# Attention rows measured over all but the last two steps of the current heads, and their transposition made a step of its own

## The chip, the cores and the metric

The kernel runs on one core of a Trainium2 chip. The metric is the device time of one execution in microseconds (us). Of an execution that was profiled, the span from the first to the last instruction of the program is known as well.

## What is computed

The reference is one layer of a hybrid decoder trunk over 1024 prompt tokens and 8 x 8 sample tokens: a norm, one input projection, sparse attention beside a gated recurrence, an output projection and a squared-ReLU MLP. The change concerns two of the three attention branches of the prompt, which the kernel runs as plain causal softmax attention (the selected blocks are all blocks here) and as a window of 512 keys, each with a linear distance bias:

```python
s = jnp.einsum('bnqgrd,bnkgd->bngrqk', qg, kb) * SCALE - slopes * dist
s = jnp.where(ok, s, NEG)
p = jax.nn.softmax(s, axis=-1)
o = jnp.einsum('bngrqk,bnkgd->bnqgrd', p, vb)
...
o_a = gates[..., 0:1] * o_cmp + gates[..., 1:2] * o_sel + gates[..., 2:3] * o_win
```

## The kernel before

The engines are named as the profile names them: PE (matrix products; PEld its weight loads), DVE (vector), ACT (activations), POOL (GpSimd) and SP (which issues DMAs). A large product is written as three products of rounded halves, hi x hi, lo x hi and hi x lo, at L136, L137 and L138.

**Groups.** A group (i, g) is one block of 128 queries (i from 0 to 7) and four of the eight heads (g is 0 or 1). There are 16, in this order: (0,0), (1,0), (2,0), (0,1), (1,1), (2,1), then (7,0), (7,1), (6,0), (6,1), (5,0), (5,1), (4,0), (4,1), (3,0), (3,1).

**Measuring.** `measure` finds, for each query row of a group, the maximum and the logarithm of the sum of its exponentials, for two branches. A step of it makes a tile of scores (PE, L841 to L846), takes its maximum (DVE, L847, tile `mxs`) and sums its exponentials (ACT, L849, tile `sms`). Its last step joins the parts (DVE L856 to L860 and ACT L858 for i of 4 and more), takes the logarithm (ACT L861), subtracts it and the gate's logarithm (DVE L862, L863), splits the result into a rounded half and the rest (DVE L866, L867, tile `rr`), transposes that (PE L869, tile `tr`) and writes it into the tile `A2` (DVE L870; the page writes it `A`). With these rows in `A2`, the products that follow give exponents that need no further normalising.

**Values.** `values` then goes over the keys of the group. Its first step transposes the small compressed probabilities (PE L907). Each further step makes scores with the keys on the partitions (PE L915, L916, at a mask L918; L916 reads `A2`), takes the exponential (ACT L920), splits it in two (L922 on ACT and DVE in turn, L923 two times in three on POOL and else on DVE), and multiplies both halves with the values into the tile `O` (PE L896, L897). These two products stand four steps back, in a queue `pend`.

**Weaving.** `attend` walks over the groups. While the value steps of a group run, the measuring steps of the next one are dealt out among them. `n0` is the number of value steps (3 for i = 0, 14 for i = 7), `n1` that of the measuring steps (3 for i = 0, 17 for i of 4 and more). After each value step and each measuring step `fill` pulls products of work that does not depend on the attention (the recurrence's output projection, then the output projection and MLP of the first 384 tokens) as PE's filling. Queries of the group after the next one are prepared at the loop's start (DVE L957 to L959) and their compressed probabilities too (PE L803, DVE L807 to L815).

**Order.** The code's order is a priority, not the order on the engines: a scheduler places each instruction by priority as soon as by its own cost model it is ready, and `fill` raises the priority of the filling. Each engine then goes through its queue strictly in the order that results. Score tiles have three PSUM banks (`SC`), `tr` has two, `O` one. After the loop, `flush` ends the queue, and the samples and the MLP follow.

Of the kernel before, what the change touches and what calls it, by code (L numbers as in the profile page):

```python
# [39 lines left out]
FEATS = ((0,), (1,), (2,), (3, 4, 5), (6, 7))  # L40
SC, TRB, MMB = 3, 2, 2
LEAD = 44
LOOK = 4
FILL0 = (2600, 0)
FILL1 = (900, 1500, 20000)
# [5 lines left out]
def trunk(ctx: ExitStack, tc: tile.TileContext, I, O):  # L51
# [12 lines left out]
    def tl(p, shape, dt=F32, tag="t", bufs=None):  # L64
        return p.tile(shape, dt, tag=tag, name=nm(tag), bufs=bufs)
# [756 lines left out]
    def measure(i, g, A1, A2):  # L822
# [30 lines left out]
        else:  # L853
# [11 lines left out]
        hi, lo = (rr[:, :, :, j].rearrange("p h b -> p b h") for j in range(2))  # L865
        V.tensor_copy(hi, nmx)  # L866
        V.tensor_tensor(lo, nmx, hi.bitcast(F32), op=ALU.subtract)  # L867
        pt = tl(ps, [128, 128], tag="tr", bufs=TRB)
        PE.transpose(pt[:16], rr.rearrange("p h b j -> p (h b j)").bitcast(F32), ident)  # L869
        V.tensor_tensor(A2[96:], pt[:16, None, :].to_broadcast([16, 4, 128]), hsel[:, :, None].to_broadcast([16, 4, 128]),  # L870
                        op=ALU.mult)
        yield

    pend = deque()

# [13 lines left out]
    def values(po, i, g, A1, A2, pcm, fill, then):  # L889
# [11 lines left out]
        for si, st in enumerate(steps):  # L901
# [22 lines left out]
            fill(0)  # L924
            later(partial(weigh, si, m, vst, ph, pl), LOOK)
            yield
# [37 lines left out]
    def attend(groups, fills, out, ready):  # L964
# [29 lines left out]
        for x, (i, g) in enumerate(groups):  # L994
            nxt = iter(())
            fill = fills[i >= NQ0]
            if x + 1 < len(groups):
                after = ready.pop(0)
                nxt = measure(*groups[x + 1], *after[:2])
                n1 = steps_of(groups[x + 1][0])  # L1000
                if x + 2 < len(groups):
                    ready.append(soon(*queries(*groups[x + 2])))
            else:
                n1 = 0
            po = lazily(lambda: tl(ps, [128, 4, 128], tag="O"))
            og = lazily(partial(place, i, g))
            work = values(po, i, g, *cur, fill, partial(finish, po, og, i, g))
            n0 = 2 * i + 3 - span(i, 1)
            done = 0
            for k in range(n0):  # L1010
                next(work, None)
                while done < n1 and (done + 1) * n0 <= (k + 1) * n1:
                    next(nxt, None)
                    fill(1)
                    done += 1
            for _ in work:
                pass
            for _ in nxt:
                fill(1)
            if x + 1 < len(groups):  # L1020
                cur = after
# [224 lines left out]
    for x, _ in enumerate(cg):  # L1246
        if x >= LEAD and x % 4 == 0:
            next(lead, None)
# [19 lines left out]
    n0, n1 = NQ0 * 128, T - NQ0 * 128  # L1268
# [218 lines left out]
```

## Time and profile before

| what | us |
|---|---|
| median of 3 timed runs | 1673.99 |
| lowest and highest of them | 1669.6, 1679.21 |
| the profiled execution | 1668.53 |
| its span, first to last instruction | 1666.9 |
| PE busy in the span | 1602.3 |
| DVE, ACT, POOL busy | 958.6, 731.0, 365.4 |

A busy PE is a PE with a product in flight; a product's own duration overlaps the next one's. The stretch of the groups lies between 455 and 935 us after the span's start. A row of the timeline gives start, duration, engine, line, operation, tiles written and read, shapes and count; the bracket at its end is the engine's idle time before it and what ended that.

### The profile page before, as it was taken

To read this page: it belongs to the slowest core of one execution; us is meant where nothing else is said; L and a number is where in the kernel's file an instruction comes from. 1 tells how busy PE (TensorE), PEld (TensorE's weight loads), DVE (VectorE), ACT (ScalarE), POOL (GpSimd) and SP (SyncE) were. 2 spreads that over 40 slices of the span, in tenths; PEclk is the share of its full clock that TensorE was granted. 3 is DMA by queue.
4 is the path that set the end of the run, shared out by engine and by line. 5 is a ranking of instruction groups with operands and counts; after the bars stand their busy time and mean duration, and the time that the engine had idled before them with its cause. 6 is when DMAs were issued, how large, how long until landed. Compare 5 with 4: busy or idle time off the path is not lost.

```text
span 1666.9 us, 26555 instructions
## 1 busy us (share of the span) xinstructions
PE 1602.3 (96%) x10009; PEld 1462.6 (88%) x10009; DVE 958.6 (58%) x1785; ACT 731.0 (44%) x1546; POOL 365.4 (22%) x322
## 2 busy tenths in 40 slices
PE   8999999998799999999999999999999999999999
PEld 6798989998677787878877778999999999999998
DVE  6245656655477888887787555565543443443442
ACT  5334544444356778666677433334321221211211
POOL 0011303304124455332233201012220120110110
PEclk9999999999799999999999999999999999999999
DMA  5332232227745332221211475445222222122222
GB/s 198 120 73 78 72 97 94 60 73 211 215 134 154 121 116 76 70 76 62 67 55 39 146 223 170 140 145 178 73 68 69 71 64 76 64 64 76 76 81 77
DMA packets 131856, 171.79 MB, mean 103 GB/s; under 512 B 33642, under 2 KB 76714, under 8 KB 131722
## 3 DMA queue, kind: packets, MB, share of 16 engines
q1 hardware_dynamic: 128810, 160.71, 31.4%
q0 software_dynamic: 2912, 9.32, 1.8%
q8 instruction: 81, 1.33, 0.3%
q14 instruction: 53, 0.43, 0.1%
HBM read 141.62 MB, written 28.84 MB: 102 GB/s over the span
## 4 chain that ended last, share of the span: by engine, by line
PE 58%; DVE 9%; issue 3%; DMA 3%; ACT 2%; SPq 2%; POOL 0%; DVEq 0%; ACTq 0%; POOLq 0%
PE mm L136 14%; PE mm L137 14%; PE mm L138 14%; DVE wl L109 2%; PE tr L915 2%; PE tr L916 1%; PE sc L286 1%; PE sc L841 1%; DVE mxs L847 1%; PE O L896 1%; PE sc L842 1%; PE O L897 1%; DMA cm<-cache_c 1%; ACT sc L849 1%; PE sc L1084 1%
## 5 line engine op out<-in xcount | busy, mean ns | idle before, releaser
L108 ACT CAST wh<-ws 128x512 fp32r<-128x512 f32 x294 | 170.1, 618 | 385.1 <-PE mm L137 271.8
L136 PE MATMUL mm<-ah,wh 128*128 128x352 f32 (+1 forms) x744 | 249.7, 336 | 0.0
L109 DVE TENSOR_TENSOR wl<-ws,wh 128x512 fp32r<-128x512 f32 x268 | 218.7, 853 | 52.4 <-ACT wh L108 51.5
L137 PE MATMUL mm<-al,wh 128*128 128x352 f32 (+1 forms) x744 | 243.5, 327 | 0.0
L138 PE MATMUL mm<-ah,wl 128*128 128x352 f32 (+1 forms) x744 | 243.2, 327 | 0.0
L136 PE MATMUL mm<-uh,wh 128*128 128x352 f32 (+1 forms) x720 | 238.6, 331 | 0.0
L138 PE MATMUL mm<-uh,wl 128*128 128x352 f32 (+1 forms) x720 | 235.2, 327 | 0.0
L137 PE MATMUL mm<-ul,wh 128*128 128x352 f32 (+1 forms) x720 | 234.8, 326 | 0.0
L1227 POOL TENSOR_TENSOR sq<-r 128x352 f32<-128x352 f32 (+1 forms) x96 | 98.8, 1029 | 561.8 <-DVE r L1225 556.4
L923 POOL TENSOR_TENSOR pl<-e,ph 128x512 fp32r<-128x512 f32 x88 | 117.1, 1336 | 210.5 <-ACT ph L922 109.0
L136 PE MATMUL mm<-X,wh 128*128 128x364 f32 (+1 forms) x480 | 162.5, 339 | 0.0
L138 PE MATMUL mm<-X,wl 128*128 128x364 f32 (+1 forms) x480 | 158.5, 330 | 3.9 <-PEq L740 3.9
L137 PE MATMUL mm<-X,wh 128*128 128x364 f32 (+1 forms) x480 | 158.5, 330 | 0.0
L137 PEld LDWEIGHTS mm<-al,wh 128*128 128x128 f32 x744 | 140.2, 188 | 4.8 <-issue 3.2
L136 PEld LDWEIGHTS mm<-ah,wh 128*128 128x128 f32 x744 | 140.8, 189 | 1.5
L138 PEld LDWEIGHTS mm<-ah,wl 128*128 128x128 f32 x744 | 139.8, 188 | 1.9 <-issue 1.6
L137 PEld LDWEIGHTS mm<-ul,wh 128*128 128x128 f32 x720 | 135.6, 188 | 2.4 <-issue 1.6
L136 PEld LDWEIGHTS mm<-uh,wh 128*128 128x128 f32 x720 | 135.9, 189 | 1.8 <-issue 0.8
L138 PEld LDWEIGHTS mm<-uh,wl 128*128 128x128 f32 x720 | 135.3, 188 | 1.6 <-issue 1.2
L1239 DVE TENSOR_TENSOR H<-H,mm 128x352 f32<-128x352 f32 (+1 forms) x90 | 47.7, 530 | 154.1 <-PE mm L138 152.4
L849 ACT ACTIVATE sc<-sc,mxs 128x320 f32<-128x320 f32 (+5 forms) x192 | 100.8, 525 | 63.0 <-DVE mxs L847 60.1
L1225 DVE SCALAR_TENSOR_TENSOR r<-mm,rs 128x352 f32<-128x352 f32 (+1 forms) x93 | 49.7, 534 | 118.2 <-PE mm L138 117.6
(408 smaller groups left out, 3309.1 us busy)
## 6 DMA issues: line engine op xcount, KB each, us to landing
ws<-w_up SPq DMA_DIRECT2D x128, 256.0 KB, 2.8
ws<-w_down SPq DMA_DIRECT2D x128, 256.0 KB, 2.9
w<-w_feat SPq DMA_DIRECT2D x40, 256.0 KB, 2.9
ws<-w_or SPq DMA_DIRECT2D x22, 256.0 KB, 3.3
w<-cmp_w SPq DMA_DIRECT2D x8, 512.0 KB, 7.0
ws<-w_oa SPq DMA_DIRECT2D x16, 256.0 KB, 3.2
pgs<-cache_s SPq DMA_DIRECT2D x32, 128.0 KB, 3.3
cw<-cwin SPq DMA_DIRECT2D x8, 512.0 KB
```

The costliest lines, as they stand in the source:

```text
L108: A.copy(wh, w)
L109: (eng or V).tensor_tensor(wl, w, wh.bitcast(F32), op=ALU.subtract)
L136: PE.matmul(p, wh, zh, start=i == 0, stop=False)
L137: PE.matmul(p, wh, zl, start=False, stop=False)
L138: PE.matmul(p, wl, zh, start=False, stop=i == n - 1)
L286: PE.matmul(ph2[:, :161], w1[w][s // 8][:, s % 8], cm[:, w, :, s], start=s == 0, stop=s == 31)
L849: A.activation(sc[:, x], sc[:, x], AF.Exp, bias=mxs[:, br, h, c:c + 1], accum_out=sms[:, br, h, c:c + 1])
L915: PE.matmul(pt, B1[:, br, g, ks], A1, start=True, stop=False)
L923: (G if turn_[0] % 3 < 2 else V).tensor_tensor(pl, e, ph.bitcast(F32), op=ALU.subtract)
L1225: V.scalar_tensor_tensor(r[:, :n], p[:, :n], 0.0, rs2[:, sl], op0=ALU.max, op1=ALU.mult)
L1227: G.tensor_tensor(sq[:, :n], r[:, :n], r[:, :n], op=ALU.mult)
L1239: V.tensor_tensor(H[:, m, sl], H[:, m, sl], p[:, :n], op=ALU.add)
```

## The change

In `measure`, the `yield` that ended the last step now stands before the transposition. So the statistics end a step, and the transposition with the write of `A2` is one more step. In `attend`, the measuring steps are dealt out over `n0 - AHEAD` value steps, with `AHEAD = 2`; `n1` still counts one step beside the score tiles, so the loop runs all up to the statistics, and the transposition is run by the `for _ in nxt` loop behind the last value step. That generator ends there without a further `yield`, so no `fill` belongs to it.

```diff
 LEAD = 44
+AHEAD = 2
 LOOK = 4
...
         V.tensor_copy(hi, nmx)
         V.tensor_tensor(lo, nmx, hi.bitcast(F32), op=ALU.subtract)
+        yield
         pt = tl(ps, [128, 128], tag="tr", bufs=TRB)
         PE.transpose(pt[:16], rr.rearrange("p h b j -> p (h b j)").bitcast(F32), ident)
         V.tensor_tensor(A2[96:], pt[:16, None, :].to_broadcast([16, 4, 128]), hsel[:, :, None].to_broadcast([16, 4, 128]),
                         op=ALU.mult)
-        yield
...
                 next(work, None)
-                while done < n1 and (done + 1) * n0 <= (k + 1) * n1:
+                while done < n1 and (done + 1) * (n0 - AHEAD) <= (k + 1) * n1:
                     next(nxt, None)
```

The changed file's line numbers are one higher, and two higher at the transposition (L871) and the write of `A2` (L872). The queues hold the same instructions as before (10591 on PE, 3846 on DVE, 1416 on ACT, 408 on POOL); only their order differs, between the first groups and the last one. Three places follow.

DVE at the end of measuring (2,0), before. `rr` is the split row, `pcm` and `mxc` are the compressed probabilities of a later group, `A_1502` is the tile that the transposition feeds:

```order
L810 TENSOR_TENSOR pcm_10186<-pcm_10186,mxc_10188 128x64
L862 TENSOR_TENSOR mxs_9999<-mxs_9999,sms_10000 128x8
L863 TENSOR_TENSOR mxs_9999<-mxs_9999,nlg_108 128x8
L812 TENSOR_REDUCE mxc_10188<-pcm_10186 128x4
L866 CAST rr_10165<-mxs_9999 128x2x4
L813 RECIPROCAL mxc_10188<-mxc_10188 128x4
L867 TENSOR_TENSOR rr_10165<-mxs_9999,rr_10165 128x2x4
L814 TENSOR_TENSOR mxc_10188<-mxc_10188,gates_107 128x4
L815 TENSOR_TENSOR pcm_10186<-pcm_10186,mxc_10188 128x64
L870 TENSOR_TENSOR A_1502_9809<-tr_10168,hsel_9470 16x512
```

The same place on DVE now (L933 adds the output of the group before into `H`, L924 splits a value step, L1165 adds the recurrence's part):

```order
L848 TENSOR_REDUCE mxs_9999<-sc_10090 128x1
L1165 TENSOR_TENSOR xr_9990<-xr_9990,mm_10075 128x384
L863 TENSOR_TENSOR mxs_9999<-mxs_9999,sms_10000 128x8
L864 TENSOR_TENSOR mxs_9999<-mxs_9999,nlg_108 128x8
L867 CAST rr_10099<-mxs_9999 128x2x4
L868 TENSOR_TENSOR rr_10099<-mxs_9999,rr_10099 128x2x4
L933 TENSOR_TENSOR H_1477_9735<-O_10034,lo_10119 64x128 x2
L924 TENSOR_TENSOR pl_10104<-e_10107,ph_10103 128x512
L1165 TENSOR_TENSOR xr_10073<-xr_10073,mm_10155 128x384
L933 TENSOR_TENSOR H_1477_9735<-O_10034,lo_10123 64x128 x2
```

Before, two rows stand between the end of `rr` and the write of `A_1502`; now sixteen do, of which the four that follow `rr` are shown.

DVE at the end of measuring (6,1), before. L1225 and L1229 belong to an MLP product of the filling, L109 splits two of its weights, and `mxs_12777` is the measuring of the group after:

```order
L847 TENSOR_REDUCE mxs_12777<-sc_12801 128x1
L1225 SCALAR_TENSOR_TENSOR r_12819<-mm_12691,rs_1478_9736 128x384
L109 TENSOR_TENSOR wl_12826<-ws_12827,wh_12825 128x512
L109 TENSOR_TENSOR wl_12826<-ws_12831,wh_12825 128x512
L1229 TENSOR_TENSOR ul_12690<-sq_12821,uh_12689 128x384
L866 CAST rr_12729<-nmx_12719 128x2x4
L813 RECIPROCAL mxc_12755<-mxc_12755 128x4
L847 TENSOR_REDUCE mxs_12777<-sc_12843 128x1
L867 TENSOR_TENSOR rr_12729<-nmx_12719,rr_12729 128x2x4
L814 TENSOR_TENSOR mxc_12755<-mxc_12755,gates_107 128x4
L815 TENSOR_TENSOR pcm_12753<-pcm_12753,mxc_12755 128x64
L932 TENSOR_TENSOR og_12865<-O_12440,lo_12866 64x128
```

The same place on DVE now (`A_2136` is the query tile of the group after, L923 and L924 are a value step of the current group):

```order
L959 TENSOR_TENSOR A_2136_12269<-stage_12266,A_2137_12270 64x512
L860 TENSOR_TENSOR sms_12306<-sms_12306,mxs_12305 128x16
L923 CAST ph_12721<-e_12726 128x512
L861 TENSOR_TENSOR smx_12691<-sms_12306 128x8
L808 TENSOR_TENSOR pcm_12753<-sc_12748,cb_12751 128x64
L924 TENSOR_TENSOR pl_12722<-e_12726,ph_12721 128x512
L863 TENSOR_TENSOR nmx_12690<-nmx_12690,smx_12691 128x8
L810 TENSOR_REDUCE mxc_12755<-pcm_12753 128x4
L864 TENSOR_TENSOR nmx_12690<-nmx_12690,nlg_108 128x8
L848 TENSOR_REDUCE mxs_12777<-sc_12779 128x1
L867 CAST rr_12700<-nmx_12690 128x2x4
L868 TENSOR_TENSOR rr_12700<-nmx_12690,rr_12700 128x2x4
```

The filling's four rows have left the stretch between the last score tile and `rr`, and query rows and a value step have come into it (one row, L811, is left out by stopping here: it stands between the last two).

PE at the end of measuring (6,1), before, from the last value products to the first value scores of (6,1):

```order
L896 MATMUL O_12440<-ph_12696,VV_9464 128x512
L897 MATMUL O_12440<-pl_12697,VV_9464 128x512
L841 MATMUL sc_12883<-B_1429_9462,A_2136_12269 128x384
L842 MATMUL sc_12883<-B_1430_9463,A_2137_12270 128x384
L869 MATMUL tr_12732<-ident_96,rr_12729 16x128
L907 MATMUL tr_12763<-ident_96,pcm_11746 16x128 x4
```

The same place on PE now:

```order
L137 MATMUL mm_12686<-ah_11552,wh_12573 128x384
L138 MATMUL mm_12686<-al_11553,wh_12573 128x384
L139 MATMUL mm_12686<-ah_11552,wl_12574 128x384
L871 MATMUL tr_12735<-ident_96,rr_12700 16x128
L908 MATMUL tr_12763<-ident_96,pcm_11746 16x128 x4
L897 MATMUL O_12449<-ph_12649,VV_9464 128x512
L898 MATMUL O_12449<-pl_12650,VV_9464 128x512
L916 MATMUL tr_12787<-A_1996_11734,B_1429_9462 128x512
L917 MATMUL tr_12787<-A_1997_11735,B_1430_9463 128x512
```

Before, four score tiles of the group after (5,0) stand ahead of the transposition; now one does, and the last two value steps of the current group stand there in their place.

## Rows read from the trace of the kernel before

**Rows 1.** The page: busy time and share of the span by engine.

```profile
PE 1602.3 (96%) x10009; PEld 1462.6 (88%) x10009; DVE 958.6 (58%) x1785; ACT 731.0 (44%) x1546; POOL 365.4 (22%) x322
```

**Rows 2.** Busy time by stretch: all groups, and groups of i from 7 to 4.

```profile
core 0: us, PE busy (x) PEld busy (x) DVE busy (x) ACT busy (x) POOL busy (x), PEclk, DMA share, GB/s
455.00:935.00 480.00, 457.22 (x2404) 373.85 (x2404) 374.75 (x832) 337.23 (x858) 178.19 (x139) 0.99 0.28 85
588.50:864.90 276.40, 265.45 (x1414) 223.83 (x1414) 222.01 (x467) 199.40 (x498) 105.02 (x82) 1.00 0.24 74
```

**Rows 3.** PE's waits from 455 to 935 us: total us, times, longest.

```profile
PE tr L869 <- DVE rr L867: 11.1, 11, 2.4
PE O L896 <- DVE og L932: 2.4, 4, 0.8
PE sc L841 <- ACT sc L849: 2.2, 3, 1.6
...
PE sc L841 <- DVE A L958: 1.0, 2, 0.5
```

**Rows 4.** Timeline of PE: the transposition at seven of the 16 groups' ends.

```profile
503.28 0.28 PE L869 MATMUL tr<-ident,rr 128*16 128x128 f32 x1 [0.94 <-DVE rr L867]
526.07 0.28 PE L869 MATMUL tr<-ident,rr 128*16 128x128 f32 x1 [0.84 <-DVE rr L867]
539.65 0.28 PE L869 MATMUL tr<-ident,rr 128*16 128x128 f32 x1 [0.80 <-DVE rr L867]
629.49 0.28 PE L869 MATMUL tr<-ident,rr 128*16 128x128 f32 x1 [2.39 <-DVE rr L867]
715.28 0.28 PE L869 MATMUL tr<-ident,rr 128*16 128x128 f32 x1 [1.50 <-DVE rr L867]
891.04 0.27 PE L869 MATMUL tr<-ident,rr 128*16 128x128 f32 x1 [1.15 <-DVE rr L867]
916.68 0.27 PE L869 MATMUL tr<-ident,rr 128*16 128x128 f32 x1 [1.12 <-DVE rr L867]
```

**Rows 5.** Timeline of PE and DVE, end of (6,1): last score product to `rr`.

```profile
704.11 0.23 PE L846 MATMUL sc<-dm 128*128 128x128 bf16 x1
704.15 0.42 PE L136 MATMUL mm<-ah,wh 128*128 128x384 f32 x1
704.41 0.34 PE L137 MATMUL mm<-al,wh 128*128 128x384 f32 x1
...
708.13 0.48 DVE L847 TENSOR_REDUCE mxs<-sc 128x1 f32<-128x320 f32 x1
708.53 0.68 DVE L923 TENSOR_TENSOR pl<-e,ph 128x512 fp32r<-128x512 f32 x1
...
715.07 0.16 DVE L867 TENSOR_TENSOR rr<-nmx,rr 128x8 fp32r<-128x8 f32 x1
```

**Rows 6.** Groups of DVE instructions from 455 to 935 us: busy us, mean ns.

```profile
L958 DVE TENSOR_TENSOR A<-stage,A 64x512 fp32r<-64x512 f32 x14 | 9.9, 710 | 0.5
L957 DVE CAST A<-stage 96x512 fp32r<-96x512 f32 x14 | 9.3, 667 | 0.0
L959 DVE CAST A<-stage 64x512 fp32r<-64x512 f32 x14 | 8.9, 633 | 1.7 <-PE tr L915 1.6
```

**Rows 7.** Timeline of DVE and POOL: three long rows of DVE, POOL beside them.

```profile
501.04 1.36 DVE L810 TENSOR_TENSOR pcm<-pcm,mxc 128x64 f32<-128x64 f32 x1
501.02 1.29 POOL L109 TENSOR_TENSOR wl<-ws,wh 128x512 fp32r<-128x512 f32 x1
524.29 1.26 DVE L863 TENSOR_TENSOR mxs<-mxs,nlg 128x8 f32<-128x8 f32 x1
524.24 1.28 POOL L923 TENSOR_TENSOR pl<-e,ph 128x512 fp32r<-128x512 f32 x1 [1.87 <-DVE mxs L862]
914.85 1.27 DVE L863 TENSOR_TENSOR mxs<-mxs,nlg 128x8 f32<-128x8 f32 x1
914.82 1.27 POOL L923 TENSOR_TENSOR pl<-e,ph 128x512 fp32r<-128x512 f32 x1 [1.40 <-DVE mxs L862]
```

**Rows 8.** One line, L867: duration ns min/median/max.

```profile
L867 DVE TENSOR_TENSOR rr<-mxs,rr x8: 159/169/176, 462.4 to 916.4; 128x8 fp32r<-128x8 f32 x8
L867 DVE TENSOR_TENSOR rr<-nmx,rr x8: 157/168/769, 588.3 to 864.7; 128x8 fp32r<-128x8 f32 x8
```

## The prediction

> **What bounds the kernel now.** The page's first part comes first: PE is busy for 96% of the span, no other engine for more than 58% [rows 1]. Then the stretch in which the change works, from 455 to 935 us: PE is busy for 457.2 of 480 us there, DVE for 374.8, ACT for 337.2 [rows 2]. So PE is the bound there too, with 22.8 us of idle time, and a change of order, which takes no product away, can win those at most. The waits of PE in that stretch say where they go: 11.1 us in 11 waits are the transposition L869 waiting for `rr` on DVE; the next kind has 2.4 us, and PE waits 1.0 us for a query tile [rows 3]. The timeline shows seven of the eleven [rows 4]; six groups' ends lie between 588 and 865 us besides the two shown, and the eight large groups (i from 7 to 4) hold together 11.1 - (0.94 + 0.84 + 0.80 + 1.15 + 1.12) = 6.25 us.
>
> Why does `rr` come late? At the end of (6,1) the last score product starts at 704.11, but DVE takes its maximum at 708.13, and `rr` ends at 715.07 + 0.16 = 715.23 [rows 5]. DVE is some 4 us behind and then needs 7.1 us for the 22 rows of its queue from that maximum to `rr`. PE has work for all but 1.50 us of it [rows 4]. In the large groups DVE is busy for 222.0 of 276.4 us, 80% [rows 2]: it is not the bound, but it is a queue.
>
> A second cause stands in single rows. L863 is a row of 8 columns, yet takes 1.26 and 1.27 us twice, and L810 1.36, each time beside a POOL row that started within 0.05 us of it and ran for some 1.28 us [rows 7]. L867 has a median of 168 ns and a longest of 769 [rows 8]. Three such rows stand just ahead of the waits of 0.94, 0.84 and 1.12 us [rows 4]: without them those waits would be nearly nothing.
>
> **What the change adds and removes.** No instruction and no DMA: every queue has the same rows in another order. Nothing is priced at its own duration, then; what counts is how far `rr` moves against the transposition. Behind a transposition that waits stand all of PE's queue and, through `A2`, the group's first scores L916. SP and POOL queues hold the same work, and behind the last group the order is the old one.
>
> **Part 1, the small groups: a gain.** At (2,0) the statistics now end with two more value steps of PE between them and the transposition; on DVE sixteen rows instead of two stand between `rr` and the write of `A2`. The rows that left DVE's way include L810, which was held for 1.36 us, and three query rows of 2.0 us [rows 6, 7]. That is more than the wait of 0.94 us, which I take off whole. At (2,1) the same happens (14 rows instead of 2), but there was no wait. At (3,0) the three query rows, 0.71 + 0.67 + 0.63 = 2.0 us [rows 6], and a value step's two move from before `rr` to behind it, against 1.15 us of wait [rows 4]: off whole. At (3,1) one row of a value step goes behind it: half of 1.12 us, 0.56. At (0,1) and (1,1) the same rows stand before `rr` as before but for two or so: nothing off. Sum: 0.94 + 1.15 + 0.56 = 2.65 us gained.
>
> **Part 2, the eight large groups: no gain.** The words of the change promise two value steps of room. The order doesn't give it, as the scheduler had made room already, from later work. Worked out at (6,1), with 0.18 us from the start of one product of 384 columns to the next, 0.24 for one of 512. Before, PE has between the last score product and the transposition 30 filling products, 8 value products, 8 score products of (5,0): 5.3 + 1.9 + 1.4, with small ones 8.7 us. Now 21 filling products, 6 value products, 5 scores of the two value steps, 2 score products: 3.7 + 1.4 + 1.2 + 0.4, some 6.8. DVE's rows from the last maximum to `rr`: 7.1 us before [rows 5]; now the filling's four rows and three maxima have gone from there, and the three query rows and a value step have come, by start-to-start times of the same trace 4.9 us. Room before: 8.7 - 7.1 = 1.6 us; now 6.8 - 4.9 = 1.9. That is the same within what I can work out, and the filling's rows now stand ahead of the maximum, where DVE was 4 us behind already.
>
> The other way to count it is the whole queue: what left PE ahead of this transposition (12 filling, 6 score, 6 value products, 4.7 us) against what left DVE ahead of `rr` (two L109, two maxima, L1225, L1229 and two small rows, 3.5 to 4.5 us). By this `rr` comes 0.2 to 1.2 us **later** against PE. At the eight ends the difference is between 0.4 and 1.2 us, 6.4 in sum. It would all be waited for only if DVE never idled; it idles for a fifth. So the term lies between 0 and +6.4 us, and I take +1.6, near the end at which DVE has idle time to catch up.
>
> **Part 3, banks and the start.** For i = 0 all measuring steps now stand behind the first value step. Only four score tiles follow there, and PE's work between a tile and the third one after it, whose bank it needs, is the same within 0.3 us at its shortest places. The waits for a score bank, 2.2 us in all [rows 3], may double: 0 to +2.2, taken as +0.
>
> **Sum.** -2.65 + 1.6 = -1.05, about -1 us on the profiled 1668.53 us (span 1666.9 and 1.6 around it): 1667.5. The median of the runs shown is 5.46 us above that execution, so I forecast 1673.
>
> **A rule of the Trainium skill.** What the rows show is a DVE row with two inputs in SBUF that lasts as long as the POOL row beside it [rows 7]. The Trainium skill, page "SBUF — State Buffer", section "Who interferes with whom", says that such a DVE instruction contends with a GpSimd instruction that reads SBUF, and that the one that was issued later is blocked for the other's whole length. By that rule, the trace agrees, the waits are collisions more than lateness; what they would make of the time is rival (c), 1677 against 1673.
>
> **Rivals.** (a) **Forecast**, lateness traded against lateness: 1673, chance 0.42.
> (b) **Room after all**: the statistics start so much earlier that DVE's idle fifth serves them, and the transposition finds `rr` ready everywhere. For it: the maxima of a group end two value steps earlier. Against: at the large ends one to four DVE rows stand between `rr` and the write of `A2`, as before (0 to 3). Price: all of 11.1 us [rows 3], 1674 - 11 = 1663. Chance 0.18.
> (c) **Collisions**: in the last stretch before `rr` there are now two value steps, whose L923 goes to POOL two times in three and lasts 1.28 us [rows 7]. Held rows cost 0.6 us (769 - 168 [rows 8]) to 1.1 (1.27 less some 0.17). If each of the eight large ends has one, at 0.9 us, that is 7.2 in place of 6.25, and the gain of part 1 is kept or lost with it: 1674 + 1 to +4, say 1677. Chance 0.14.
> (d) **Nothing moves**, the scheduler's new order is as good as the old: 1674. Chance 0.11.
> (e) **Slower, by the query rows**: L957 to L959 wait for the last value scores of the current group, since query tiles have two buffers, and now stand between the last maximum and `rr` at nine ends from (7,0) to (3,0) or so. PE's next score products L841 need L958, and waited 1.0 us for it twice before [rows 3]; `rr` needs DVE behind it. If DVE is late by its old 4 us when it reaches them, PE waits first at L841 and then at L869 for what is left of the 2.0 us [rows 6]. It decides from where L958 ends after PE has reached that L841. Price: 9 x 2.0 = 18 us at most; half of it is likely, since the old waits are part of it: +9, 1683. Chance 0.15.
>
> **How the numbers follow.** Within 0.5%, 8.4 us, is about what a measurement of this kernel can tell from no change. (a), (c) and (d) are within it, 0.67; (b) is faster by more, with half a microsecond's doubt on each side, 0.18; (e) slower by more, 0.15. The median runs of one kernel spread from 1669.6 to 1679.2. The range takes in (b) at its price and (e) to its price, 1663 to 1682, and leaves out the half of each that lies beyond.
>
> **What would show it.** Right: the wait L869 for `rr` falls from 11.1 to between 8 and 12 us; none at (2,0), little at (3,0); waits of some 1 us remain at most of the large ends; DVE's rows there go from the query tiles to `rr` without idle time. (b): that wait under 3 us and PE's idle time in the groups' stretch under 13. (c): long L856 to L867 rows ahead of the waits that remain. (e): the wait L841 for L958 above 5 us. The forecast is wrong if PE's busy time outside the groups' stretch moves, since I hold it fixed.

## The result, and the profile after

The changed kernel takes 1690.3 us (median of 6 runs, 1688.3 to 1693.0), the kernel before 1669.7 us beside it. The ratio is 1.0114, with a 95% interval of 1.0096 to 1.0132: slower by 1.1%, outside the predicted range. The profiled execution took 1688.36 us with a span of 1686.4, 19.5 us more than the span before.

In the code after, `rr` is at L868, the transposition at L871, the query rows at L958 to L960, the score products at L842, the split of `e` at L924, POOL's other split at L110.

The page's first part, and the stretch of the groups (columns as in [rows 2]):

```profile
PE 1611.6 (96%) x9983; PEld 1468.9 (87%) x10009; DVE 968.7 (57%) x1785; ACT 730.9 (43%) x1546; POOL 367.1 (22%) x322
...
455.00:935.00 480.00, 445.01 (x2303) 364.55 (x2326) 375.30 (x812) 326.36 (x835) 172.66 (x133) 0.98 0.28 84
```

PE is idle for 480 - 445.0 = 35.0 us there, against 22.8 [rows 2]: 12.2 us more. The mean granted clock of the execution fell from 0.990 to 0.986, so the time lost to the clock rose from 1666.9 x 0.010 = 16.7 to 1686.4 x 0.014 = 23.6 us: 6.9 more. Together 19.1 of the 19.5 us. (The last transposition comes at 933.2 us now, 916.7 before, so the stretch holds a little less of the same work; up to 955 us PE's idle time is 36.1.) PE's waits from 455 to 960 us (total us, times, longest; to be held against [rows 3]):

```profile
PE sc L842 <- DVE A L959: 9.1, 7, 2.1
PE tr L871 <- DVE rr L868: 7.9, 8, 1.8
PE O L897 <- DVE og L933: 4.0, 5, 1.7
PE O L897 <- DVE H L933: 2.4, 3, 1.1
PE O L897 <- ACT sc L850: 2.0, 2, 1.2
...
PE tr L871 <- DVE mxc L815: 1.2, 1, 1.2
...
PE tr L871 <- DVE mxc L813: 0.6, 1, 0.6
```

The transposition waits nearly as before (7.9 + 1.2 + 0.6 = 9.7 against 11.1). New is the wait of the first score products for the query rows, 9.1 against 1.0, and the waits for the write of `O`, whose tile DVE must first empty. Four of these waits on PE's timeline, at the ends of (7,1), (6,1) and (5,1):

```profile
624.53 0.45 PE L842 MATMUL sc<-B,A 128*128 128x448 f32 x1 [1.43 <-DVE A L959]
627.13 0.27 PE L871 MATMUL tr<-ident,rr 128*16 128x128 f32 x1 [1.76 <-DVE rr L868]
715.96 0.55 PE L842 MATMUL sc<-B,A 128*128 128x384 f32 x1 [2.06 <-DVE A L959]
797.61 0.38 PE L842 MATMUL sc<-B,A 128*128 128x320 f32 x1 [1.61 <-DVE A L959]
```

What DVE did around the first two, and POOL beside it:

```profile
619.87 1.08 DVE L858 TENSOR_TENSOR mxs<-nmx,mxs 128x16 f32<-128x16 f32 x1
...
623.70 0.69 DVE L959 TENSOR_TENSOR A<-stage,A 64x512 fp32r<-64x512 f32 x1
624.42 1.13 DVE L864 TENSOR_TENSOR nmx<-nmx,nlg 128x8 f32<-128x8 f32 x1
...
625.61 1.17 DVE L867 CAST rr<-nmx 128x8 fp32r<-128x8 f32 x1
...
623.81 2.93 POOL L924 TENSOR_TENSOR pl<-e,ph 128x512 fp32r<-128x512 f32 x2 [1.92 <-DVE ph L923]
```

Two statistics rows of 8 columns, some 0.17 us each in their undisturbed form, take 1.13 and 1.17 us, and each ends with one of the two POOL rows of the value steps. Without that `rr` would have been ready 2.0 us earlier, more than the 1.76 us that PE waited; and L858, held as well, stands ahead of the query row that PE awaited first. Such rows are more frequent than before: of the statistics rows (L857 to L868) between 455 and 945 us, 16 last over 0.5 us, ten of them beside an L924; before it was 8, five beside an L923. Their whole busy time rose from 21.4 to 30.8 us. The same happens to a query row at the end of (5,1), ahead of the wait at 797.61:

```profile
794.07 1.52 DVE L958 CAST A<-stage 96x512 fp32r<-96x512 f32 x1
795.51 1.23 DVE L860 TENSOR_TENSOR sms<-sms,mxs 128x16 f32<-128x16 f32 x1
...
793.81 2.91 POOL L924 TENSOR_TENSOR pl<-e,ph 128x512 fp32r<-128x512 f32 x2 [5.70 <-DVE mxs L858]
```

### The profile page after: what moved, and what is told of

Its sections match the earlier page's. It is cut to its first block, busy times and chain, and to the rows that moved or that the text cites. A ratio compares the mean times of both kernels' runs of the same rounds, so it can differ in the third digit from the quotient of the medians.

```text
span 1686.4 us, 26566 instructions
## 1 busy us (share of the span) xinstructions
PE 1611.6 (96%) x9983; PEld 1468.9 (87%) x10009; DVE 968.7 (57%) x1785; ACT 730.9 (43%) x1546; POOL 367.1 (22%) x322
## 4 chain that ended last, share of the span: by engine, by line
PE 53%; DVE 10%; issue 4%; DMA 4%; ACT 4%; SPq 1%; POOL 1%; DVEq 0%; POOLq 0%; ACTq 0%
PE mm L137 14%; PE mm L139 14%; PE mm L138 14%; DVE wl L110 2%; DVE mxs L848 1%; PE sc L287 1%; ACT sc L850 1%; PE tr L916 1%; DMA cm<-cache_c 1%; PE sc L842 1%; PE O L897 1%; PE tr L917 1%; PE sc L843 1%; PE O L898 1%; ACT wh L109 1%
## 5 line engine op out<-in xcount | busy, mean ns | idle before, releaser
L109 ACT CAST wh<-ws 128x512 fp32r<-128x512 f32 x294 | 170.5, 618 | 390.0 <-PE mm L138 275.8
L110 DVE TENSOR_TENSOR wl<-ws,wh 128x512 fp32r<-128x512 f32 x268 | 221.2, 861 | 53.1 <-ACT wh L109 52.4
L924 POOL TENSOR_TENSOR pl<-e,ph 128x512 fp32r<-128x512 f32 x88 | 118.3, 1347 | 251.0 <-ACT ph L923 118.5
L850 ACT ACTIVATE sc<-sc,mxs 128x320 f32<-128x320 f32 (+5 forms) x192 | 100.9, 526 | 56.5 <-DVE mxs L848 54.6
```

The costliest lines, as they stand in the source:

```text
L109: A.copy(wh, w)
L110: (eng or V).tensor_tensor(wl, w, wh.bitcast(F32), op=ALU.subtract)
L850: A.activation(sc[:, x], sc[:, x], AF.Exp, bias=mxs[:, br, h, c:c + 1], accum_out=sms[:, br, h, c:c + 1])
L924: (G if turn_[0] % 3 < 2 else V).tensor_tensor(pl, e, ph.bitcast(F32), op=ALU.subtract)
```

## The experiments

By the waits alone the query rows, rival (e), are the cause (theory Q): their wait has grown by 8.1 us. The runs were made to test that against three others: the pacing as such (theory P), DVE's load at the ends (theory D), and rows of DVE held beside POOL, rival (c) (theory G).

The numbers of all of them stand in one table. "PE idle" is that from 455 to 935 us (the expectations reckon partly to 960 us, which adds about 1 us). "Held" is worked out from the trace: for all rows of DVE from the last maximum of a group to its `rr`, what each lasts beyond the lower quartile of its own kind, summed over the ends of the eight large groups. The time also moves with the granted clock, which in the runs of the kernel before alone lay between 0.980 and 0.993; so "span x clock", the mean over a kernel's runs, is the nearest thing to a time at full clock. The ratio is that to the kernel before on the same chip.

| kernel | median us | ratio (95%) | PE idle | held | span x clock |
|---|---|---|---|---|---|
| before | 1669.7 to 1674.6 | 1 | 22.8 | 8.8 | 1649 to 1650 |
| changed | 1690.3 | 1.0114 (1.0096 to 1.0132) | 35.0 | 15.6 | 1663.8 |
| two_after | 1695.6 | 1.0154 (1.0120 to 1.0188) | 35.7 | 15.6 | 1663.7 |
| three_after | 1690.7 | 1.0122 (1.0088 to 1.0155) | 32.9 | 15.0 | 1657.5 |
| three_before | 1684.7 | 1.0053 (1.0027 to 1.0079) | 27.0 | 8.7 | 1653.5 |
| e3_ahead_only | 1678.8 | 1.0034 (1.0011 to 1.0058) | 26.8 | 5.8 | 1659.2 |
| e5_ahead1 | 1678.6 | 1.0029 (1.0005 to 1.0053) | 28.9 | 12.6 | 1656.4 |
| off_three_after | 1692.3 | 1.0096 (1.0066 to 1.0127) | 34.7 | 22.0 | 1659.3 |
| off_three_before | 1690.1 | 1.0101 (1.0079 to 1.0124) | 31.1 | 13.3 | 1659.1 |
| fill_after | 1697.0 | 1.0132 (1.0105 to 1.0160) | 34.6 | 17.9 | 1674.0 |
| nopool_after | 1670.9 | 0.9998 (0.9978 to 1.0018) | 19.4 | 4.1 | 1649.2 |
| nopool_before | 1670.4 | 1.0000 (0.9978 to 1.0022) | 19.4 | 6.0 | 1649.8 |
| nopool_three_after | 1676.7 | 1.0026 (1.0003 to 1.0050) | 21.2 | 4.4 | 1647.7 |
| light_after | 1672.3 | 1.0015 (0.9991 to 1.0040) | 21.4 | 3.5 | 1648.1 |
| dummy_nopool_after | 1696.9 | 1.0146 (1.0098 to 1.0193) | 34.7 | 14.6 | 1667.1 |
| dummymid_nopool_after | 1679.3 | 1.0051 (1.0022 to 1.0080) | 24.5 | 4.1 | 1654.3 |
| poolend_before | 1692.8 | 1.0119 (1.0072 to 1.0167) | 30.8 | 10.5 | 1663.3 |
| nopool_ahead1 | 1670.8 | 0.9992 (0.9973 to 1.0011) | 19.9 | 6.0 | 1650.5 |

### The query rows: three buffers

```diff
-        st = tl(aq, [96, 4, 128], tag="stage", bufs=3)
+        st = tl(aq, [96, 4, 128], tag="stage", bufs=2)
...
-        A1 = tl(aq, [128, 4, 128], F32R, tag="A1", bufs=2)
-        A2 = tl(aq, [112, 4, 128], F32R, tag="A2", bufs=2)
+        A1 = tl(aq, [128, 4, 128], F32R, tag="A1", bufs=3)
+        A2 = tl(aq, [112, 4, 128], F32R, tag="A2", bufs=3)
...
-        qp = tl(aq, [128, 2, 128], tag="pairs", bufs=3)
+        qp = tl(aq, [128, 2, 128], tag="pairs", bufs=2)
```

In the changed kernel (three_after), in the one before (three_before), and, as a control, the changed kernel with the lines of `stage` and `pairs` alone (two_after).

> The changed kernel with three buffers instead of two for the query tiles A1 and A2; to make room, two buffers instead of three for stage and pairs. The order of PE's products at the ends of the large groups stays that of the changed kernel (2.0 to 2.6 us of PE work, by the columns of the products, between the last value scores of a group and the first score products of the group after next), but the three query rows no longer wait for those value scores and stand 47 to 81 DVE rows ahead of rr instead of up to 14. Theory Q (the query rows, by their two buffers, are the cause): PE's wait at L842 for L959, 9.1 us in 7 waits in the changed kernel, is nearly gone (under 1 us), PE's idle time in the groups' stretch falls from 35.0 to under 24 us, the stretches of half clock there go with it, and the time is 1668 to 1674 us, 0.990 of the changed kernel's or less. Theory P (the new pacing as such delays rr, with the query rows or without): L842 has no wait, but the transposition's wait for rr grows by what L842 lost; time 1684 to 1690. Theory G (collisions of DVE rows with POOL rows): as the changed kernel, 1686 to 1692.

> The kernel before with the same edit: three buffers for A1 and A2, two for stage and pairs. Before, PE has 4.0 to 5.0 us of work between those two places and waits 1.0 us for the query rows. Theory Q: little to gain there, but the three rows (2.0 us) also leave DVE's queue between the last maximum and rr, so the 11.1 us of waits for rr may fall by some us: 1664 to 1670. Theories P and G: 1668 to 1672, no change.

> Control: the changed kernel with two buffers instead of three for stage and pairs, and the query tiles as they are. In the groups with i from 7 to 3 the order is the changed kernel's. All theories: 1688 to 1693 us, as the changed kernel; anything else is the price of the room, to be taken from the run with three query buffers.

Theory Q falls, by its own numbers. The wait for the query rows went, but PE's idle time fell only from 35.7 to 32.9 us, and the time from 1695.6 to 1690.7. (The control, two_after, lies above its forecast of 1688 to 1693; its interval overlaps that of the changed kernel.) The waits of three_after at the transposition:

```profile
PE tr L871 <- DVE rr L868: 9.4, 6, 3.1
PE tr L871 <- DVE pcm L808: 6.3, 2, 3.7
PE tr L871 <- DVE mxc L814: 2.5, 1, 2.5
...
PE tr L871 <- DVE mxc L813: 1.4, 1, 1.4
...
PE tr L871 <- DVE mxc L810: 1.2, 1, 1.2
```

The releasers named at L808 to L814 are DVE rows that stand directly beside `rr` in its queue, so these five lines are one kind of wait: 20.8 us in place of 9.7. DVE was late, and PE waited for it at whichever of the two products it came to first. Theory P had forecast just this, with a time of 1684 to 1690 us (1690.7 measured), and theory G's time fits as well; the run doesn't tell these two apart. Where PE waits does not say why DVE is late.

three_before missed all its forecasts (1664 to 1672): the edit alone costs the kernel before 0.5%, with no more held time (8.7 us). Its waits for the tiles that must be emptied ahead of `O` are 7.1 us in place of 3.5; what brings them isn't settled.

### Which half of the change, and how much of it

Only the pacing, in the kernel before (e3_ahead_only), and the changed kernel with a lead of one step (e5_ahead1):

```diff
-                while done < n1 and (done + 1) * n0 <= (k + 1) * n1:
+                while done < n1 and (done + 1) * (n0 - 2) <= (k + 1) * n1:
```

```diff
-AHEAD = 2
+AHEAD = 1
```

> Only the pacing: the kernel before with its measuring steps paced to end two value steps early, the transposition still in the last measuring step. (The other half alone, the yield moved at the old pace, leaves all but 34 of PE's 9656 rows where they are, and is not run.) By the order PE then has 1.5 to 2.0 us between the last value scores and the first score products of the group after next, and these and the query rows stand behind the transposition, no longer ahead of rr. Theory Q: L841 waits for the query rows still, 1 to 2 us at each of nine ends, 9 to 18 us, because their room is even smaller than in the changed kernel; the wait for rr may stay at 8 to 12 us; time 1680 to 1692, slower than before. Theory P': the harm is done by the query rows standing ahead of rr: here they stand behind it, so the wait for rr falls and the time is at most that of before, 1660 to 1670.

> The changed kernel with a lead of one value step in place of two. By the order PE's work between the last value scores and the first score products of the group after next is 2.0 to 2.6 us at most ends, as with a lead of two, and 3.6 at one. Theories Q and D: most of the loss is there already, 1682 to 1690, span times clock 1658 to 1663. Theory P: half the packing, half the loss, 1676 to 1682, span times clock 1654 to 1658.

By the ratio each loses a quarter to a third of what the change loses; by span x clock it is more, 9.9 and 7.4 us of some 14. e3_ahead_only lies between the ranges of its two theories. e5_ahead1 speaks against Q and D, which wanted most of the loss with a lead of one, and comes where theory P had it (1676 to 1682, span x clock 1654 to 1658). The query rows' wait is 4.3 us in e3_ahead_only, where their room is smallest, against the 9 to 18 expected: a second sign against Q. In e3_ahead_only DVE's rows are held for 5.8 us only, so its 0.3% comes from something else, which these runs don't settle.

### DVE's load at the ends

With the buffers of three_after, in the changed kernel and in the one before:

```diff
-        V.tensor_copy(A2[:96], st)
-        V.tensor_tensor(A1[64:], st[:64], A2[:64].bitcast(F32), op=ALU.subtract)
-        V.tensor_copy(A1[:64], st[:64])
+        A.copy(A2[:96], st)
+        G.tensor_tensor(A1[64:], st[:64], A2[:64].bitcast(F32), op=ALU.subtract)
+        A.copy(A1[:64], st[:64])
```

> The changed kernel with three buffers for the query tiles (two for stage and pairs), and the three query rows taken off DVE: the two casts on ACT, the difference on POOL. Theory D (between the last maximum of a group and the first one of the next DVE has more work than PE, and PE waits for what is left over, whichever wait it meets first): there DVE was busy all of 53.0 us at the eight large groups' ends, against 14.7 before, and PE idle for 10.4 us there, against 0.0; with 2.0 us of rows taken off each end, PE's idle time at the ends falls from 9.7 us (three buffers alone) to under 3, its idle time in the groups' stretch from 34.1 to 18 to 26 us, and the waits for rr from 20.8 to under 13. The time at full clock (span times granted clock), 1657.5 us with three buffers alone, falls to 1645 to 1652; the time to 1668 to 1680. Theory P (the maxima packed into fewer value steps make DVE late all along the group): the dense part's idle time of 11.3 us stays and so does most of the wait for rr: span times clock 1654 to 1658, time 1682 to 1690.

> The kernel before with the same two edits. Theory D: before, PE was idle for nothing in the short part between the last maximum and the next first one, so DVE's 2.0 us less there are worth little: span times clock 1648 to 1654, time 1668 to 1680. If it gains as much as the changed kernel does, DVE's load as such is what counts, not where the change puts it.

Theory D falls too: 2.0 us of DVE's work less at each end, and nothing gained; the kernel before, with the same edits, is 1.0% slower than without (0.5% with the buffers alone). The statistics rows offer a reason. In off_three_after 27 of them last over 0.5 us, and their busy time is 41.9 us in place of 31.6 (three_after). DVE and POOL at the end of (5,0), in front of a wait of 3.9 us:

```profile
764.46 1.20 DVE L863 TENSOR_TENSOR nmx<-nmx,smx 128x8 f32<-128x8 f32 x1 [0.28 <-ACT smx L862]
...
766.10 1.25 DVE L868 TENSOR_TENSOR rr<-nmx,rr 128x8 fp32r<-128x8 f32 x1
...
764.36 1.27 POOL L924 TENSOR_TENSOR pl<-e,ph 128x512 fp32r<-128x512 f32 x1 [2.81 <-ACT ph L923]
766.06 1.25 POOL L959 TENSOR_TENSOR A<-stage,A 64x512 fp32r<-64x512 f32 x1 [0.44 <-ACT A L958]
```

The difference that was moved to POOL now holds `rr` itself. This run was the hint that rival (c) had been set aside too early.

### The clock

```diff
+FILL = 8
...
                     edge = br == 1 and i >= 4 and c == 0
+                    if i >= 4 and br == 0 and h0 == 0 and c == 0:
+                        for _ in range(FILL):
+                            PE.matmul(sc[:, 0], dm[:, 2], VV[:, 0].bitcast(BF16).rearrange("p a b d -> p (a b d)")[:, :n], start=True, stop=True, skip_group_check=True)
```

> The changed kernel with eight products more (128 rows by 320 to 512 columns, into a score bank that the first score product then overwrites) ahead of the first score product of each group with i from 7 to 4: 1.1 to 1.7 us of PE work that nothing needs, eight times. Theory C (the stretches of half clock follow PE's waits of 1.5 to 2 us): PE is busy where it waited for the query rows, the wait at L842 for L959 falls from 9.1 to under 3 us, and the stretches of half clock at 627, 716 and 798 us (13.6 us together, some 7 us of time) are gone; the time is 1680 to 1690, as the changed kernel or less, although PE has 9 to 13 us more to do. If the clock has nothing to do with the waits, the stretches stay and the time is 1690 to 1700.

Not decided. The products did fill the wait for the query rows (9.1 to 1.2 us), and the stretches of half clock at 716 and 798 us went; but waits of 3.1 and 3.5 us came up at the transposition instead, at 589 and 634 us, each again with a stretch of 3.4 us at half clock beside it, and the sum stayed 20.5 us. The kernel is slower than the changed one by 6.7 us, and the added products alone had been reckoned at 9 to 13. What remains of theory C is what the rows of the changed kernel show (last section).

### POOL's rows away from the ends

```diff
-                (G if turn_[0] % 3 < 2 else V).tensor_tensor(pl, e, ph.bitcast(F32), op=ALU.subtract)
+                (V if si >= len(steps) - 3 or turn_[0] % 6 == 0 else G).tensor_tensor(pl, e, ph.bitcast(F32), op=ALU.subtract)
```

In the changed kernel (nopool_after), the one before (nopool_before), and with three buffers (nopool_three_after); light_after also has this:

```diff
-                (A.copy if turn_[0] % 2 else V.tensor_copy)(ph, e)
+                (A.copy if turn_[0] % 2 or si >= len(steps) - 3 else V.tensor_copy)(ph, e)
```

> The changed kernel; the difference pl of the last three value steps of each group always on DVE, and in exchange only every sixth of the others (two of three went to POOL before, in all steps), so that DVE has about as many of these rows as before, but POOL none near a group's end. In the changed kernel sixteen of the short statistics rows L857 to L868 (0.15 to 0.2 us each) last over 0.5 us beside a POOL row, ten of them beside an L924; before, there are eight, five of them beside an L923; at the eight large ends that is 9.0 us of held time against 3.7. Theory G (these held rows make rr and the query rows late): the held rows fall to eight or fewer, PE's idle time in the groups' stretch falls by 3 to 8 us from 35.0, and the time is 1679 to 1686. Theory Q (the query rows' two buffers alone): the wait at L842 stays at 7 us or more and the time at 1686 to 1693. Against a gain: DVE has two rows of 0.7 us more at each end.

> The kernel before with the same edit, as a control. Theory G: half as much to win, 0 to 4 us, 1666 to 1675; theory Q: no change, 1668 to 1678. If it loses 4 us or more, DVE's rows at the end weigh more than the held time.

> The changed kernel with both: three buffers for the query tiles (two for stage and pairs), and pl placed as in the run before. With three buffers alone the wait at L842 went, but the waits at the transposition rose to 20.8 us, since DVE was late there by as much. Theories Q and G together (two causes, of which either alone leaves the other's wait): the wait for rr falls to 8 to 14 us, the idle time in the groups' stretch to 22 to 28, span times clock from 1657.5 to 1648 to 1654, and the time to 1670 to 1682. If G plays no part: waits at the transposition stay at 18 us or more, 1686 to 1693.

> The changed kernel with pl placed as in nopool_after, and the copy ph of the last three value steps always on ACT (every second one was on DVE, 0.4 to 1.0 us each). DVE gives up 1 or 2 rows at each end, and ACT, busy for half of the time between the last maximum of a group and the first of the next, takes them. If DVE's queue at the end is the limit, PE's idle time falls by another 3 to 6 us against nopool_after: 1674 to 1683. If ACT's exponentials are late by what it takes over, no gain or a loss: 1683 to 1692.

This gives the whole loss back, more than theory G had asked for (1679 to 1686): 1670.9 us, while the same edit does nothing for the kernel before. The pacing is still that of the changed kernel, so theory P can't be the whole of it. The stretch and two waits of nopool_after:

```profile
455.00:935.00 480.00, 460.58 (x2392) 376.52 (x2416) 367.89 (x847) 337.24 (x862) 165.04 (x135) 0.99 0.28 86
...
PE sc L842 <- DVE A L959: 1.6, 3, 1.0
...
PE tr L871 <- DVE rr L868: 1.0, 2, 0.7
```

The waits for the query rows and for `rr` have both gone, with two buffers and the lead of two. Theory Q had the wait at L842 stay at 7 us or more. At the end of (6,1) PE's order around the last maximum is the same in both kernels, and DVE's nearly so; the changed one has

```profile
709.80 2.40 DVE L110 TENSOR_TENSOR wl<-ws,wh 128x512 fp32r<-128x512 f32 x2
709.91 1.74 POOL L924 TENSOR_TENSOR pl<-e,ph 128x512 fp32r<-128x512 f32 x1 [0.36 <-DVE ph L923]
711.92 1.41 POOL L924 TENSOR_TENSOR pl<-e,ph 128x512 fp32r<-128x512 f32 x1 [0.27 <-ACT ph L923]
...
712.12 1.63 DVE L1230 TENSOR_TENSOR ul<-sq,uh 128x384 fp32r<-128x384 f32 x1
713.68 0.47 DVE L848 TENSOR_REDUCE mxs<-sc 128x1 f32<-128x320 f32 x1
...
715.13 0.69 DVE L959 TENSOR_TENSOR A<-stage,A 64x512 fp32r<-64x512 f32 x1
```

and nopool_after, where POOL has no row from 700.75 to 709 us and PE's L842 at 705.58 waits for nothing,

```profile
699.99 1.92 DVE L110 TENSOR_TENSOR wl<-ws,wh 128x512 fp32r<-128x512 f32 x2
701.83 0.55 DVE L1230 TENSOR_TENSOR ul<-sq,uh 128x384 fp32r<-128x384 f32 x1
702.30 0.68 DVE L924 TENSOR_TENSOR pl<-e,ph 128x512 fp32r<-128x512 f32 x1
702.90 0.48 DVE L848 TENSOR_REDUCE mxs<-sc 128x1 f32<-128x320 f32 x1
...
704.75 0.69 DVE L959 TENSOR_TENSOR A<-stage,A 64x512 fp32r<-64x512 f32 x1
705.58 0.41 PE L842 MATMUL sc<-B,A 128*128 128x384 f32 x1
```

So the wait of 2.06 us for a query row has rows of the filling behind it that were held ahead of the last maximum: L110 and L1230 last 1.6 us longer here than in nopool_after. That isn't all of it. DVE also comes to these rows 1.4 us later against PE's products than in nopool_after, and has two rows of `pl` fewer behind them (1.35 us).

The edit thus does more than take rows from POOL. With `pl` on DVE the scheduler also finds another order: at the eight large ends PE has 128,544 columns of products between a group's last score product and its transposition in place of 109,024, some 9 us more at 0.18 us for 384, while DVE has some 10 us more of rows there. The two about cancel, but the order isn't that of the changed kernel. The next runs leave the order alone.

Three buffers and a lighter DVE add nothing (1676.7 and 1672.3 us, the second below both its forecasts; PE's idle time 21.2 and 21.4): once DVE's rows aren't held, neither the room for the query rows nor DVE's queue is what ends last.

### Held rows, or a late `pl`?

The edit also computes `pl` on the faster engine, 0.69 us in place of 1.35. So POOL's rows were put back without their result being used:

```diff
                 (V if si >= len(steps) - 3 or turn_[0] % 6 == 0 else G).tensor_tensor(pl, e, ph.bitcast(F32), op=ALU.subtract)
+                if si >= len(steps) - 3 and turn_[0] % 3 < 2:
+                    G.tensor_tensor(tl(pp_, [128, 4, 128], BF16, tag="idle"), e, ph.bitcast(F32), op=ALU.subtract)
```

For dummymid_nopool_after the condition is `len(steps) - 9 <= si < len(steps) - 6 and turn_[0] % 3 < 2`. poolend_before has `G if si >= len(steps) - 3 or turn_[0] % 7 < 4 else V` in the kernel before, and nopool_ahead1 is nopool_after with `AHEAD = 1`.

> nopool_after with 30 more rows on POOL: in the last three value steps of each group, two times in three, POOL computes the same difference of e and ph once more, into a tile that nobody reads. The order of PE, of DVE and of ACT is that of nopool_after, row for row; only POOL has more to do, at the places where the changed kernel had its L924 rows. Theory G (DVE rows held beside POOL rows make rr and the query rows late): statistics rows over 0.5 us rise from 5 to 10 or more, PE's idle time in the groups' stretch from 20.3 us to 27 to 36, and the time from 1671 to 1679 to 1692. Theory L (what hurt in the changed kernel was that pl came late from POOL, 1.35 us a row against 0.7 on DVE, and with it the last value products and the end of the group): pl is on DVE here as in nopool_after, so nothing comes back: 1668 to 1675.

> The same additional POOL rows, but in the third of the value steps before that, away from the ends (19 rows, none in the groups with few steps); again PE's order is that of nopool_after. Theory G: the place counts, not POOL's load: maxima and casts are held in mid-group, where DVE has time, so 1670 to 1677 and idle time of 20 to 25 us. If POOL's load or the scratch rows as such cost, the time is that of dummy_nopool_after.

> The kernel before, with the opposite edit: pl of the last three value steps of each group always on POOL, and four of seven of the others, so that POOL has about as many rows as before, but more of them at the ends. Theory G: the kernel before is made to lose as the changed kernel did: held statistics rows rise from 8 to 11 to 16, the wait for rr from 11.1 to 14 to 20 us, time 1676 to 1690. If the changed kernel's loss needs its own order (room of 2.0 to 2.6 us in place of 4.0 to 5.0) to show, 1668 to 1676.

> nopool_after with a lead of one value step in place of two. With the old placing of pl a lead of one gave 1678.5 us and a lead of two 1690.3; with pl moved a lead of two gives 1670.9, as before. Theory G: what made the lead harmful is gone, so one and two are alike within 5 us: 1666 to 1676; a time under 1665 would be faster than both kernels.

The two runs with unused POOL rows are the clean ones. In the traces of dummy_nopool_after the rows of PE, DVE and ACT stand in the same order as in nopool_after; only POOL has more. The 30 rows cost 26 us, more than theory G had forecast (1679 to 1692), and theory L falls. At the eight large ends DVE needs 66.0 us from the last maximum to `rr` in place of 56.1, as much more as its rows are held longer (14.6 against 4.1 us). PE waits 2.5 us for POOL's own results (1.7 in nopool_after), so little of the cost is POOL's results being late. (PE's idle time rose by 15.3 us in the stretch; the clock, reckoned as above, took 8.8 us more of the profiled execution.) The changed kernel's waits come back in the same shape:

```profile
PE sc L842 <- DVE A L961: 10.3, 7, 2.2
PE tr L871 <- DVE rr L868: 6.0, 5, 2.4
```

and so do its held rows; here at the end of (7,1), whose `rr` PE then awaits for 1.97 us:

```profile
629.59 1.13 DVE L864 TENSOR_TENSOR nmx<-nmx,nlg 128x8 f32<-128x8 f32 x1
631.25 1.25 DVE L867 CAST rr<-nmx 128x8 fp32r<-128x8 f32 x1
...
628.98 3.49 POOL L926 TENSOR_TENSOR idle<-e,ph 128x512 bf16<-128x512 f32 x2 [1.92 <-DVE ph L923]
```

At the same place of nopool_after the two rows take 0.17 us each, and the transposition at 624.40 doesn't wait. 19 such rows in mid-group cost 8 us, a little over the 1670 to 1677 expected. By the row that is 0.4 us against 0.9 at the ends: the place counts, though not alone. The ends are untouched here (held 4.1 us, the transposition's wait 1.0 us); part of the cost is POOL being late itself:

```profile
PE O L897 <- DVE og L935: 4.8, 5, 1.2
PE mm L1195 <- POOL hsq L1192: 3.8, 1, 3.8
```

The second of these is 1.2 us in nopool_after. The kernel before, too, can be made to lose 1.2% by the placing of `pl`: poolend_before has 12 held statistics rows, and

```profile
PE tr L869 <- DVE rr L867: 18.0, 13, 3.5
```

in place of 11.1 [rows 3]. Its counts are those that theory G forecast, its time is above (1676 to 1690). But the loss is not shown to be that of held rows: held time rose only from 8.8 to 10.5 us, and the order changed with the edit, so that PE has 65,760 columns of products between a large group's last maximum and its transposition in place of 87,552. With POOL's rows out of the way a lead of one and of two give the same time, 1670.8 and 1670.9. No version was faster than the kernel before beyond the interval.

## Why the prediction was wrong, point by point

**What bounds the kernel** was read rightly: PE is the bound, DVE a queue. PE's busy time outside the stretch about held as well: 1147.7 us outside 455 to 955, against 1145.1 outside 455 to 935 before.

**Part 1** (-2.65 us) did not come. The wait at (2,0) fell from 0.94 to 0.11 us and that at (3,1) from 1.12 to 0, as forecast; but at (3,0) it stayed, 1.20, since two statistics rows there were held (L864 for 1.28, L867 for 1.20 us). From the first transposition to that of (7,0) both kernels take 123 us.

**Part 2** (+1.6) is the step that failed. Its count of rows was good: at (6,1) DVE takes 4.5 us from the last maximum to the end of `rr`, where 4.9 had been worked out, and over the eight large ends PE's work from the last maximum to the transposition is 54.6 us less 9.1 of new waits, 45.5, against 44.8. But it priced DVE's rows at the durations of the old trace, as if these belonged to the rows and not to what runs beside them. From the last maximum to `rr` DVE needs 60.5 us at the eight ends in place of 50.7; of these 9.8 us, 15.6 - 8.8 = 6.8 are held time, nearly all of it beside POOL rows; the rest lies in which rows stand there, for DVE's idle time is 2.2 us (2.5 before). The transposition's waits there sum to 7.1 us (6.25 before), and 9.1 us came at L842. An estimate from the two traces: if at no end PE could win back more than the time held there, held rows would account for at most 8.0 of the 10.0 us by which these waits grew. How much it is in the changed kernel's own order no run isolates. At (6,1) itself none of it lies where the sum was made: the rows from the last maximum on were not held (0.1 us), and the wait of 2.06 us came from DVE being late at that maximum.

**Rival (c)**, collisions, had the right mechanism with a chance of 0.14 and a price of +1 to +4 us. Two things were wrong in it. It let held rows take the place of the old waits, where they add to a queue that PE's work covers, by the prediction's own count, with 1.6 to 1.9 us to spare at an end. And it counted only rows between the statistics and `rr`, where the held row can be any row of DVE's queue, the query rows and the filling's among them. So POOL's rows should have been laid beside DVE's whole queue in the new order, and not beside `rr` alone. The Trainium skill, page "SBUF — State Buffer", section "Who interferes with whom", says that a DVE instruction with two inputs in SBUF contends with a GpSimd instruction that reads SBUF, and calls the contention an exclusive lock. The traces agree: L864 at the end of (7,1) ends at 625.55 us, the POOL row beside it at 625.52; at (6,1) the row held beside a POOL row was L1230 of the filling.

**Rival (e)**, the query rows, looks right by the waits: 9.1 us at L842, its +9. The runs take that back. With the third buffer the wait went and the time hardly moved; with DVE's rows no longer held the wait went, though nothing was done for the query rows' buffers. The wait was where the lateness showed.

**Rival (b)**, room after all, shows in nopool_after: with POOL's rows away from the ends the transposition waits 1.0 us in all and PE is idle for 19.4 us. It gains no time, though, since the kernel before gets to the same 19.4 us by the same edit.

**The clock** was left out. By the reckoning above it accounts for 6.9 of the 19.5 us, and the range, whose upper end was built on waits alone, did not have it.

## What to carry over

When an order changes, lay the rows of POOL beside those of DVE in the new order before durations are taken from the old trace: a row of 0.17 us can last 1.2 beside a POOL row, and it counts wherever PE waits behind that queue. The tile that PE waits for tells where the lateness surfaces, not what caused it; a run that removes the wait but not the time says to look further back. A row of POOL that nobody waits for, added at one place and then at another with all other queues left as they are, is a cheap and clear test of this; moving a row to another engine changes the order of the others too.

## What the runs showed of the hardware

Some waits of 1.4 to 2.1 us on PE were followed by stretches at a granted clock of half (1.2 in place of 2.4 GHz) in which PE was busy again. In the changed kernel these come with the waits at 624.5 and 627.1 (1.43 and 1.76 us), at 716.0 (2.06), at 797.6 and 798.9 (1.61 and 0.94) and at 919.8 us (1.68, for `O`); the third column from the end is the granted clock:

```profile
627.30:630.70 3.40, 3.40 (x13) 3.04 (x12) 2.90 (x7) 2.92 (x8) 0.00 (x0) 0.51 0.08 18
716.10:719.50 3.40, 3.40 (x14) 2.87 (x14) 2.61 (x12) 1.03 (x4) 0.00 (x0) 0.50 0.40 110
798.00:804.80 6.80, 5.87 (x20) 5.01 (x21) 4.33 (x15) 2.05 (x5) 0.00 (x0) 0.50 0.14 36
920.90:924.30 3.40, 3.40 (x9) 2.49 (x10) 3.17 (x6) 1.10 (x4) 0.60 (x1) 0.50 0.25 80
```

It is no fixed price: the wait of 2.02 us at 758.3 was followed by none, and in the kernel before neither was that of 2.39 us [rows 4]. In the groups' stretch half-clock time rose from 6.8 to 20.5 us, of which about half is lost. In the 18 profiled kernels together, from 455 to 960 us, such a stretch began between 1 us before and 4 us after the end of 20 of the 31 waits of 2 to 3 us, but only of 12 of the 51 waits of 1.2 to 1.6 us. Whether the waits bring the clock down was not isolated, since fill_after moved the waits instead of removing them.

Casts with one input were held like the rows with two: L867 for 1.17 and 1.25 us, L958 for 1.52, each beside a POOL row.
